# A hybrid decoder block: the products that spread the shares of the attention's groups, as pairs on half the array rows, two chunks at once

## Chip, cores and metric

The kernel runs on one core of one Trainium2 chip. The metric is the device time of one execution in microseconds, the median of three runs. The core has five engines, each with an instruction queue of its own that is worked in order: TensorE (PE, matrix products), VectorE (DVE), ScalarE (ACT), GpSimd (POOL) and SyncE (SP), which here only issues DMAs.

## The reference

One decoder layer in float32 over a sequence of 2048 positions and a width of 1024. The part that matters here is the combination of the attention's three groups, which differ in window and dilation:

```python
for g, (window, dilation) in enumerate(DILATION_GROUPS):        # (128,1), (512,4), (2048,16)
    o_g, lse_g = dilated_band_attention(q[:, :, g], k[:, :, g], v[:, :, g], window, dilation)
...
wts = jax.nn.softmax(jnp.stack(lses, axis=0), axis=0)           # over the groups: the shares
attn = jnp.sum(wts[..., None] * jnp.stack(outs, axis=0), axis=0)
attn = attn.reshape(B, S, ATTN_OUT_WIDTH).astype(dt) * jax.nn.silu(g_attn)
y_a = attn @ w_attn_proj[l]
```

Each of the 8 heads of a group has 64 channels. Beside it a second branch (convolution, gated recurrence) ends in `y_b = (h * silu(g_lru)) @ w_lru_proj`; both are gated, added, projected and normalised.

## The kernel before

The program has three stages: the input projection up to about 1450 us, the attention to 1775 us, and the output projections to the end. The change lies in the attention.

**Work of the attention.** Heads go in four pairs (`hp` 0 to 3), each with three units, one for each group of the reference. The 12 units have 16 blocks of 128 queries. The loop `for G in range(NG + 1)` takes four blocks a turn (`scores(2G)` and `scores(2G+1)`, two blocks each), so a unit lasts four turns. The text calls a turn of this loop a group, and "short" one where the blocks have no previous block of keys: 8 transposes in a turn of p instead of 16, and scores 128 wide instead of 192.

In a group, in this order: `turn_p(2G-2)` transposes the p of the group before on PE and `copy_p` brings the result from PSUM to SBUF (half e=0 by ACT, half e=1 by DVE); `scores(2G)` multiplies q and k on PE; `weigh` masks and takes the minimum on DVE, then the exponential on ACT; `scores(2G+1)`; `turn_p(2G-1)` with its copies; two more `weigh`; `values` (PE, into o) with a copy by DVE; then prefetches (`todo`). The rest of the group is filled with a product of the other branch: `yb_part(n, hf, 0..3)`, 3 products each, half an output tile yb a group. When the second half ends, `yb_done` multiplies it into gB on DVE. Groups 20 and 37 have no yb (`rests`). In every fourth group `turn_ml` transposes the minima and sums (tile mlt, PSUM buffer o).

**Shares.** When a head pair's three units are done, `weights(hp)` works out the shares from the tiles mt, on DVE, ACT and POOL, in steps set for the groups e+1 to e+4 (e is 12, 24, 36 for hp 0, 1, 2), and stores 12 rows of 2048 in DRAM (`w_scr`). In group e+6 `load_wh` fetches them, one chunk of 512 positions a DMA, into `WH[c % 2]`, which holds two chunks each.

**Spreading.** The share of a head has to stand on that head's 64 partitions. `spread(hp, c, g, tag)` does it by a product with a 0/1 matrix `sel`, 128 x 128 on 512 columns, float32r, into a PSUM tile w; DVE multiplies o by it, and one group later POOL adds (`join`), and for the last of the three g multiplies by the gate ga and stores to `at_scr`. Each head pair has 4 chunks and 3 groups g, 12 products. For hp 0 to 2 the table `spreads` sets them into the groups from e+7 on, two a group, between parts of yb, with the PSUM tags s0 and s1 that the scores have too (two buffers each). hp 3 follows in the last stage, with tag z.

**Buffers and queues.** The order on each engine is the order of the calls. The tile pool makes whoever takes a buffer wait for the last reader of what was in it. ga tiles and the raw weights wlr share six buffers (tag rc), loaded through SP's queue.

Of the kernel before, what the change touches and what calls it, by code (L numbers as in the profile page):

```python
# [8 lines left out]
F32 = mybir.dt.float32  # L9
# [6 lines left out]
P = 128  # L16
# [4 lines left out]
CH = 512  # L21
# [10 lines left out]
def hybrid_block_kernel(ctx: ExitStack, tc: tile.TileContext, a: dict, out: bass.AP):  # L32
    nc = tc.nc
    sp, act, dve, pool, pe = nc.sync, nc.scalar, nc.vector, nc.gpsimd, nc.tensor

    def flat(t):
        return t.bitcast(F32)
# [6 lines left out]
    w_scr = [dram.tile([12, S], F32, name=f"w_scr{hp}") for hp in range(HP)]  # L44
# [59 lines left out]
    cur = {}  # L104
# [8 lines left out]
    def later(lag, fn):  # L113
        late.append((now["n"] + lag, fn))
# [4 lines left out]
    def run(queue):  # L119
        due = [x for x in queue if x[0] <= now["n"]]  # L120
        queue[:] = [x for x in queue if x[0] > now["n"]]
        for _, fn in due:
            fn()
# [21 lines left out]
    ps = stA.enter_context(tc.tile_pool(name="ps", bufs=2, space=PSUM))  # L145
# [93 lines left out]
    def tt(eng, out, in0, in1, op):  # L239
        eng.tensor_tensor(out=out, in0=in0, in1=in1, op=op)  # L240
# [70 lines left out]
    lo_, up_ = slice(0, 64), slice(64, P)  # L311
# [263 lines left out]
    base = [sum(ticks[:s]) for s in range(NQ + 1)]  # L575
# [137 lines left out]
    for s, pl in enumerate(plan):  # L713
        if pl[0] and pl[4] == "ug":
            i = pl[1][1][0] - FT_U
# [210 lines left out]
    sel = w_p.tile([P, 2, 3, P], F32R, name="sel")  # L926
    WH = [w_p.tile([P, CH], F32R, name=f"wh{i}") for i in range(2)]
# [3 lines left out]
    aps = stB.enter_context(tc.tile_pool(name="aps", bufs=2, space=PSUM, reuse_waits="tile"))  # L931
# [3 lines left out]
    def rc(name):  # L935
        return rc_p.tile([P, CH], F32, tag="rc", name=name, bufs=6)
# [17 lines left out]
    def selectors():  # L954
        for r in range(2):
            t = rc(f"self{r}")[:, 0:3 * P].rearrange("p (g f) -> p g f", g=3)
            pool.memset(t, 0.0)
            for g in range(3):
                for x in range(2):
                    v = t[:, g].rearrange("p (h f) -> p h f", h=2)  # L960
                    pool.affine_select(out=v, in_=v, pattern=[[-1, 2], [0, 64]], compare_op=ALU.not_equal, fill=1.0,
                                       base=-(32 * r + 6 * x + 2 * g), channel_multiplier=1)
            pool.tensor_copy(sel[:, r], t)
        for w in WH:
            pool.memset(flat(w), 0.0)
# [65 lines left out]

    def copy_p(j, e):
        ptb, pt, los = st["t", j]
        on_act = e == 0 or (j % 2 and (j + 1) // 2 in spreads)
        whole = los[0] == los[1]
        for b in (slice(0, 2),) if whole else (slice(0, 1), slice(1, 2)):
            lo = los[b.start]
            dst, src = ptb[:, b, :, 64 * e:64 * e + 64], pt[e][:, b]
            if lo:
                dst, src = (t.rearrange("p b (h x) f -> p b h x f", x=2)[:, :, :, 1, :] for t in (dst, src))  # L1040
            if on_act:
                act.activation(dst, src, AF.Copy)
            else:
                dve.tensor_copy(dst, src)
# [100 lines left out]
        return top, sums, lambda: (shares(), store())  # L1145

    def load_wh(hp, c):
        sp.dma_start(flat(WH[c % 2][32 * (c // 2):32 * (c // 2) + 12]), w_scr[hp][:, c * CH:(c + 1) * CH])

    def spread(hp, c, g, tag):  # L1150

        cs = slice(c * CH, (c + 1) * CH)
        os = [o_tile(3 * hp + UG[x])[:, cs] for x in range(3)]
        w = cur["ps"].tile([P, CH], F32, tag=tag, name=f"w{hp}{c}{g}", bufs=cur["wb"])
        pe.matmul(w, sel[:, c // 2, g], WH[c % 2], start=True, stop=True)
        tt(dve, os[g], os[g], w, ALU.mult)
        if g == 0:
            st["ga", hp, c] = rc(f"ga{hp}{c}")
            sp.dma_start(st["ga", hp, c], ga_scr[hp * P:(hp + 1) * P, cs])
            return  # L1160

        def join():
            tt(pool, os[0], os[0], os[g], ALU.add)
            if g == 1:
                tt(pool, os[0], os[0], st.pop(("ga", hp, c)), ALU.mult)
                if hp == 3 and c == CO[0]:
                    later(1, lambda: split(AT[c][:, 3, 0], AT[c][:, 3, 1], os[0]))
                else:
                    pool.dma_start(at_scr[hp * P:(hp + 1) * P, cs], os[0])

        later(1, join)
# [146 lines left out]
    for hp in range(3):  # L1318
        e = 4 * (3 * hp + 2) + 4
# [8 lines left out]
    spreads = {}  # L1328
    for hp in range(3):
        e = 4 * (3 * hp + 2) + 4  # L1330
        for i in range(12):
            c, g = i // 3, (0, 2, 1)[i % 3]
            spreads.setdefault(e + 7 + (i + (hp < 2)) // 2, []).append((hp, c, g))

    rests = set()
    for G in range(NG + 1):
        run(late)
        if G < NG:
            if G:
                turn_p(2 * G - 2)  # L1340
                copy_p(2 * G - 2, 0)
                copy_p(2 * G - 2, 1)
            scores(2 * G)
            weigh(4 * G)
            weigh(4 * G + 1)
            scores(2 * G + 1)
            if G:
                turn_p(2 * G - 1)
                copy_p(2 * G - 1, 0)
                copy_p(2 * G - 1, 1)  # L1350
            weigh(4 * G + 2)
# [12 lines left out]
        for fn in todo.pop(G, ()):  # L1364
            fn()
        y = G >= GY and G not in rests and (G < NG or len(halves) % 2)
        if y:
            n, hf = divmod(halves[0], 2)
            yb_part(n, hf, 0)
            yb_part(n, hf, 1)  # L1370
        two = spreads.pop(G, [])
        if len(two) == 2:
            spread(*two[0], "s0")
        if y:
            yb_part(n, hf, 2)
        if two:
            spread(*two[-1], "s1")
        if y:
            yb_part(n, hf, 3)
            if hf:  # L1380
                yb_done(n)
        if G % 4 == 0 and G:
            turn_ml(G // 4 - 1)
        if y:
            yb_care(halves.pop(0))
            if hf and n in (7, 15):
                rests.add(G + 1)
        now["n"] += 1
# [203 lines left out]
    for t, tt in enumerate(TT):  # L1592
        c, b = divmod(t, 4)
# [67 lines left out]
```

## Time and profile before

| | |
|---|---|
| median of 3 runs | 2114.13 us (2111.71 to 2115.91) |
| profiled execution, first to last instruction (the only time listed for it) | 2110.6 us |
| PE busy | 2092.4 us, 99% |
| DVE busy | 1645.0 us, 78% |
| ACT busy | 1212.7 us, 57% |
| POOL busy | 764.2 us, 36% |
| granted TensorE clock, mean | 0.998 |
| chain that ended last | PE 95%, DMA 2%, DVE 1%, POOL 1%, ACT 1% |
| spreading products in the attention, L1155 | 36, mean 401 ns, busy 14.1 us |
| multiplications by them on DVE | 36, median 687 ns |

A row of the order in time is: start in us, duration in us, engine, line, operation, output <- inputs, the operand's rows and columns, shape, count. Consecutive instructions of one kind are merged into one row, whose duration reaches from the first start to the last end. Matmuls overlap, so what one costs is the step from start to start. In brackets stands the idle time of the engine just before, and what ended it.

### The profile page before, as it was taken

To read this page: it belongs to the slowest core of one execution; us is meant where nothing else is said; L and a number is where in the kernel's file an instruction comes from. 1 tells how busy PE (TensorE), PEld (TensorE's weight loads), DVE (VectorE), ACT (ScalarE), POOL (GpSimd) and SP (SyncE) were. 2 spreads that over 40 slices of the span, in tenths; PEclk is the share of its full clock that TensorE was granted. 3 is DMA by queue.
4 is the path that set the end of the run, shared out by engine and by line. 5 is a ranking of instruction groups with operands and counts; after the bars stand their busy time and mean duration, and the time that the engine had idled before them with its cause. 6 is when DMAs were issued, how large, how long until landed. Compare 5 with 4: busy or idle time off the path is not lost.

```text
span 2110.6 us, 35731 instructions
## 1 busy us (share of the span) xinstructions
PE 2092.4 (99%) x12069; PEld 1713.1 (81%) x12069; DVE 1645.0 (78%) x2937; ACT 1212.7 (57%) x2510; POOL 764.2 (36%) x685
## 2 busy tenths in 40 slices
PE   9999999999999999999999999999999999999998
PEld 7888888888888888888888888887888878788886
DVE  8878988989988868677777878875667776877667
ACT  6456556567567556677677787775666664321100
POOL 1544653653653301111111111112547678521120
PEclk9999999999999999999999999999999999999999
DMA  7876976886886866566665666669879886774431
GB/s 222 245 230 196 266 227 203 255 239 208 248 256 210 301 192 181 191 205 174 206 190 175 207 205 204 188 205 275 209 208 260 233 234 184 243 243 154 152 100 70
DMA packets 259205, 443.10 MB, mean 210 GB/s; under 512 B 65504, under 2 KB 92160, under 8 KB 255952
## 3 DMA queue, kind: packets, MB, share of 16 engines
q1 hardware_dynamic: 242384, 408.38, 62.0%
q0 software_dynamic: 11744, 23.54, 6.0%
q10 hardware_dynamic: 4896, 8.92, 1.1%
q8 instruction: 96, 1.57, 0.3%
q14 instruction: 85, 0.70, 0.1%
HBM read 289.74 MB, written 150.99 MB: 209 GB/s over the span
## 4 chain that ended last, share of the span: by engine, by line
PE 95%; DMA 2%; DVE 1%; POOL 1%; ACT 1%; issue 1%; SPq 0%; ACTq 0%; POOLq 0%; DVEq 0%
PE q L639 65%; PE yb L1231 6%; PE o L1061 3%; PE z L1536 3%; PE z L1537 3%; PE z L1538 3%; PE pt L1029 2%; PE s L998 2%; PE ya L1504 1%; PE ya L1503 1%; PE ya L1505 1%; PE g L500 1%; PE vtp L370 1%; PE s L992 1%; DMA war<-in_w_f_dram 1%
## 5 line engine op out<-in xcount | busy, mean ns | idle before, releaser
L639 PE MATMUL q<-xT,hS 128*128 128x512 f32 x1632 | 505.0, 391 | 0.1
L639 PE MATMUL q<-xT,l 128*128 128x512 f32 x1088 | 423.5, 389 | 0.0
L639 PE MATMUL q<-xB,hA 128*128 128x512 f32 x1344 | 418.0, 392 | 0.0
L639 PE MATMUL q<-xB,l 128*128 128x512 f32 x944 | 367.9, 390 | 0.0
L639 PEld LDWEIGHTS q<-xT,hS 128*128 128x128 f32 x1632 | 304.6, 188 | 65.0 <-issue 2.7
L639 PEld LDWEIGHTS q<-xB,hA 128*128 128x128 f32 x1344 | 250.7, 188 | 57.0 <-issue 5.8
L639 PEld LDWEIGHTS q<-xT,l 128*128 128x128 f32 x1088 | 204.3, 188 | 42.6
L240 POOL TENSOR_TENSOR sw<-sw,sin 128x512 f32<-128x512 f32 x96 | 156.8, 1639 | 166.2 <-ACT sw L329 94.7
L639 PEld LDWEIGHTS q<-xB,l 128*128 128x128 f32 x944 | 177.5, 188 | 37.2
L240 POOL TENSOR_TENSOR y<-y,h 128x512 f32<-128x512 f32 x28 | 38.8, 1386 | 384.1 <-DVE h L541 352.1
L1014 ACT ACTIVATE pb<-pb 128x192 f32<-128x192 f32 (+1 forms) x384 | 160.7, 422 | 26.5 <-DVE pb L1012 26.4
L639 PE MATMUL q<-xB,hS 128*128 128x512 f32 x544 | 169.0, 392 | 0.0
L639 PE MATMUL q<-xT,hA 128*128 128x512 f32 x544 | 167.8, 390 | 0.0
L284 ACT ACTIVATE hA<-wA 128x512 fp32r<-128x512 f32 x220 | 138.6, 636 | 28.5 <-DVE l L240 9.1
L1231 PE MATMUL yb<-hx,wl 128*128 128x512 f32 x576 | 148.9, 400 | 0.1
L284 ACT ACTIVATE hS<-S 128x512 fp32r<-128x512 f32 x170 | 108.6, 639 | 60.7 <-DVE S L240 47.3
L240 POOL TENSOR_TENSOR l<-wA,hA 128x512 fp32r<-128x512 f32 x68 | 107.8, 1585 | 91.4 <-ACT hA L284 60.9
L1231 PEld LDWEIGHTS yb<-hx,wl 128*128 128x128 f32 x576 | 104.8, 188 | 28.4 <-issue 5.6
L639 PEld LDWEIGHTS q<-xT,hA 128*128 128x128 f32 x544 | 101.9, 188 | 21.4 <-issue 0.4
L639 PEld LDWEIGHTS q<-xB,hS 128*128 128x128 f32 x544 | 101.2, 188 | 21.5 <-issue 1.1
L240 DVE TENSOR_TENSOR S<-S,wA 128x512 f32<-128x512 f32 x102 | 96.8, 949 | 11.5 <-DMA wA<-in_w_in_dram 7.9
L1507 POOL TENSOR_TENSOR me<-gA,me 128x512 f32<-128x512 f32 x30 | 47.7, 1607 | 157.6 <-DVE gA L1506 135.3
(213 smaller groups left out, 4325.4 us busy)
## 6 DMA issues: line engine op xcount, KB each, us to landing
wA<-in_w_in_dram SPq DMA_DIRECT2D x220, 256.0 KB
wl_scr<-l SPq DMA_DIRECT2D x102, 512.0 KB
l<-wl_scr SPq DMA_DIRECT2D x102, 512.0 KB
wS<-in_w_in_dram SPq DMA_DIRECT2D x102, 256.0 KB
wS<-in_w_in_dram POOLq DMA_DIRECT2D x68, 256.0 KB, 7.0
wlr<-in_w_f_dram SPq DMA_DIRECT2D x64, 256.0 KB
mg_scr<-y SPq DMA_DIRECT2D x59, 256.0 KB
v_scr<-vs SPq DMA_DIRECT2D x48, 256.0 KB
```

The source lines that it names most:

```text
L240: eng.tensor_tensor(out=out, in0=in0, in1=in1, op=op)
L284: act.activation(heads(h), heads(r, False), AF.Copy)
L639: pe.matmul(bank, w[:, ks], x[:, kk, xx], start=(first and i == 0), stop=(last and i == 11))
L998: pe.matmul(bank[h][es, b, 0:BW], q[hs, n * P + 64 * e:n * P + 64 * e + 64], k_[hs, at + 64 * e:at + 64 * e + BW], start=True, stop=True)
L1014: act.activation(pp, pp, AF.Exp, scale=-1.0, bias=mm, accum_out=ll)
L1029: pe.transpose(pt[e][:, b, 2 * h + x, :], pdata(p, h, c, c + P)[hs], ident[hs, hs])
L1061: pe.matmul(o[hs, 2 * i + b, :], V[:, kb, 64 * h:64 * h + 64], ptb[:, b, 2 * h + x, :], start=(x == lo // P), stop=(x == 1))
L1231: pe.matmul(YB["t"], w[:, a, k], hx(8 * c + k)[:, b], start=(hf == 0 and m == 0), stop=(hf == 1 and m == 11))
L1507: (dve if i in (6, 7) else pool).tensor_tensor(out=ME[c][:, f], in0=ga, in1=ME[c][:, f], op=ALU.add)
L1536: pe.matmul(z, mh[:, k], w[:, 0, hs], start=(k == 0), stop=False)
L1537: pe.matmul(z, mh[:, k], w[:, 1, hs], start=False, stop=False)
L1538: pe.matmul(z, ml[:, k], w[:, 0, hs], start=False, stop=(k == 7))
```

## The change

```diff
             pool.affine_select(out=v, in_=v, pattern=[[-1, 2], [0, 64]], compare_op=ALU.not_equal, fill=1.0,
-                               base=-(32 * r + 6 * x + 2 * g), channel_multiplier=1)
+                               base=-(64 * r + 6 * x + 2 * g), channel_multiplier=1)
...
-        on_act = e == 0 or (j % 2 and (j + 1) // 2 in spreads)
+        on_act = e == 0 or (j % 2 and (j + 1) // 2 in shared)
...
     def load_wh(hp, c):
-        sp.dma_start(flat(WH[c % 2][32 * (c // 2):32 * (c // 2) + 12]), w_scr[hp][:, c * CH:(c + 1) * CH])
+        sp.dma_start(flat(WH[c % 2][64 * (c // 2):64 * (c // 2) + 12]), w_scr[hp][:, c * CH:(c + 1) * CH])
...
+    def spread_pair(hp, c, g):
+
+        ws = [aps.tile([P, CH], F32, tag=f"s{r}", name=f"w{hp}{c + 2 * r}{g}", bufs=2) for r in range(2)]
+        for r, hs in enumerate((lo_, up_)):
+            pe.matmul(ws[r], sel[hs, r, g], WH[c][hs], start=True, stop=True)
+        for r in range(2):
+            share(hp, c + 2 * r, g, ws[r])
...
-        for i in range(12):
-            c, g = i // 3, (0, 2, 1)[i % 3]
-            spreads.setdefault(e + 7 + (i + (hp < 2)) // 2, []).append((hp, c, g))
+        for i in range(6):
+            spreads[e + 7 + i + (hp < 2)] = (hp, i // 3, (0, 2, 1)[i % 3])
+    shared = set(spreads)
...
     for G in range(NG + 1):
         run(late)
+        if G in spreads:
+            spread_pair(*spreads.pop(G))
...
-        two = spreads.pop(G, [])
-        if len(two) == 2:
-            spread(*two[0], "s0")
-        if y:
             yb_part(n, hf, 2)
-        if two:
-            spread(*two[-1], "s1")
-        if y:
             yb_part(n, hf, 3)
```

`share` is what `spread` did after its product: the multiplication, the load of ga for g = 0, and the join. The rows of the second chunk in a WH tile move from partition 32 to partition 64, and with them the ones in `sel`. So chunks c and c+2 lie on the two halves of the array rows, and one pair of products, 64 rows each, spreads both. There are 6 pairs for each of hp 0 to 2. They stand in the groups 20 to 25, 32 to 37 and 43 to 48, each ahead of the first turn of p; the products stood in the groups 19 to 25, 31 to 37 and 43 to 48.

PE around the end of group 22 and the start of group 23. In a name like w011 the digits are hp, chunk and g; pt044 is half 0 of the turn of scores 44. Before:

```order
L1231 MATMUL yb10_16245<-hx1_13981,wl_13979 128x512 x6
L1155 MATMUL w011_16380<-wh1_13984,sel_13982 128x512
L1231 MATMUL yb10_16245<-hx1_13981,wl_13979 128x512 x3
L1155 MATMUL w020_16386<-wh0_13983,sel_13982 128x512
L1231 MATMUL yb10_16245<-hx1_13981,wl_13979 128x512 x3
L1029 MATMUL pt044_16401<-ident_161,pb_13978 128x64
```

After:

```order
L1061 MATMUL o41_16353<-ptb42_16277,V_13900 64x128 x8
L1243 MATMUL yb10_16246<-hx1_13981,wl_13979 128x512 x12
L1160 MATMUL w010_16396<-wh1_13984,sel_13982 128x512
L1160 MATMUL w030_16397<-wh1_13984,sel_13982 128x512
L1029 MATMUL pt044_16406<-ident_161,pb_13978 128x64
```

The two products left the middle of yb and stand as a pair of chunks 1 and 3 behind it, directly ahead of the turn, and so ahead of the scores of group 23.

DVE at the same place, from the copy of o in group 22 to the first weigh of group 23 (s046). Before:

```order
L1077 COPY o1_13976<-o41_16353 128x2x128 x2
L240 TENSOR_TENSOR o1_13976<-o1_13976,w011_16380 128x512
L240 TENSOR_TENSOR o2_13977<-o2_13977,w020_16386 128x512
L1241 SCALAR_TENSOR_TENSOR gB8_16072<-gB8_16072,yb10_16245 128x512
L1044 COPY ptb44_16403<-pt144_16402 128x8x64
L1012 ISA pb_13978<-s046_16422,band_171 128x192
```

After:

```order
L1077 COPY o1_13976<-o41_16353 128x2x128 x2
L1253 SCALAR_TENSOR_TENSOR gB8_16067<-gB8_16067,yb10_16246 128x512
L240 TENSOR_TENSOR o2_13977<-o2_13977,w010_16396 128x512
L240 TENSOR_TENSOR o2_13977<-o2_13977,w030_16397 128x512
L1044 COPY ptb44_16408<-pt144_16407 128x8x64
L1012 ISA pb_13978<-s046_16427,band_171 128x192
```

The two multiplications moved behind the one into gB, between it and the copy of the turn.

POOL from the last join of hp 1 to the weights of hp 2 (mt2), groups 38 and 39; ga13 is the gate of hp 1, chunk 3. Before:

```order
L240 TENSOR_TENSOR o0_13975<-o0_13975,o1_13976 128x512
L240 TENSOR_TENSOR o0_13975<-o0_13975,ga13_18000 128x512
L1169 DMA at_scr_74<-o0_13975 128x512
L1190 CAST wl_13979<-wlr170_17874 128x512
L240 TENSOR_TENSOR wl_13979<-wlr170_17874,wl_13979 128x512
L1190 CAST wl_13979<-wlr171_17875 128x512
L240 TENSOR_TENSOR wl_13979<-wlr171_17875,wl_13979 128x512
L240 TENSOR_TENSOR mt2_17316<-whl2_18138,mt2_17316 32x128
```

After:

```order
L240 TENSOR_TENSOR o0_13975<-o0_13975,o1_13976 128x512
L240 TENSOR_TENSOR o0_13975<-o0_13975,ga11_17754 128x512
L1181 DMA at_scr_74<-o0_13975 128x512
L240 TENSOR_TENSOR o0_13975<-o0_13975,o1_13976 128x512
L240 TENSOR_TENSOR o0_13975<-o0_13975,ga13_17757 128x512
L1181 DMA at_scr_74<-o0_13975 128x512
L1202 CAST wl_13979<-wlr170_17873 128x512
L240 TENSOR_TENSOR wl_13979<-wlr170_17873,wl_13979 128x512
L1202 CAST wl_13979<-wlr171_17874 128x512
L240 TENSOR_TENSOR wl_13979<-wlr171_17874,wl_13979 128x512
L240 TENSOR_TENSOR mt2_17316<-whl2_18138,mt2_17316 32x128
```

The joins of chunks 1 and 3 now follow each other here; chunk 1's stood three groups earlier.

More of the change, by code (lines that the diff above doesn't have):

```diff
@@ L1147, in load_wh, with share @@
     def load_wh(hp, c):
-        sp.dma_start(flat(WH[c % 2][32 * (c // 2):32 * (c // 2) + 12]), w_scr[hp][:, c * CH:(c + 1) * CH])
+        sp.dma_start(flat(WH[c % 2][64 * (c // 2):64 * (c // 2) + 12]), w_scr[hp][:, c * CH:(c + 1) * CH])
     def spread(hp, c, g, tag):
+        w = cur["ps"].tile([P, CH], F32, tag=tag, name=f"w{hp}{c}{g}", bufs=cur["wb"])
+        pe.matmul(w, sel[:, c // 2, g], WH[c % 2], start=True, stop=True)
+        share(hp, c, g, w)
+    def spread_pair(hp, c, g):
[4 more added lines that the diff above has]
+            share(hp, c + 2 * r, g, ws[r])
+    def share(hp, c, g, w):
         cs = slice(c * CH, (c + 1) * CH)
         os = [o_tile(3 * hp + UG[x])[:, cs] for x in range(3)]
-        w = cur["ps"].tile([P, CH], F32, tag=tag, name=f"w{hp}{c}{g}", bufs=cur["wb"])
-        pe.matmul(w, sel[:, c // 2, g], WH[c % 2], start=True, stop=True)
         tt(dve, os[g], os[g], w, ALU.mult)
```

## The prediction

> **What bounds the kernel now.** First the page's head, then the busy time by stretch, then the waits of TensorE, and only then the order of time inside the attention, where the change acts.
>
> ```profile
> span 2110.6 us, 35731 instructions
> PE 2092.4 (99%) x12069; PEld 1713.1 (81%) x12069; DVE 1645.0 (78%) x2937; ACT 1212.7 (57%) x2510; POOL 764.2 (36%) x685
> 1655.00:1705.00 50.00, 49.95 (x673) 40.35 (x668) 38.32 (x157) 35.97 (x145) 35.12 (x37) 1.00 0.95 257
> PE mlt L1082 <- DVE o L1077: 0.6, 1, 0.6
> PE pt L1029 <- ACT ptb L1042: 2.3, 3, 1.5
> ```
>
> TensorE (PE) is the bound. The third line is a stretch in the middle of the changed groups (its columns: window, length, then busy time and count of PE, weight loads, VectorE, ScalarE, GpSimd, then PE's granted clock, the DMA share, GB/s): PE is busy 49.95 of 50 us while VectorE (DVE) is busy 38.3. The last two lines are all that PE waited for DVE's and ACT's copies in the whole attention. So a product taken from PE is worth its slot, and every new wait of PE costs its full length. The sum stands against the span of 2110.6 us; the median of the runs is 2114.13, so 3.5 us lie around the span, and I add the difference to the median.
>
> Two whole groups as PE runs them, one with two spreading products, one with none, then the starts of a short group and of the group that lacks yb:
>
> ```profile
> 1592.01 1.67 PE L1231 MATMUL yb<-hx,wl 128*128 128x512 f32 x6
> 1593.52 0.39 PE L1155 MATMUL w<-wh,sel 128*128 128x512 f32 x1
> 1593.75 0.86 PE L1231 MATMUL yb<-hx,wl 128*128 128x512 f32 x3
> 1594.45 0.39 PE L1155 MATMUL w<-wh,sel 128*128 128x512 f32 x1
> 1594.68 0.84 PE L1231 MATMUL yb<-hx,wl 128*128 128x512 f32 x3
> 1595.45 0.71 PE L1029 MATMUL pt<-ident,pb 64*128 64x64 f32 x16
> 1596.09 1.53 PE L998 MATMUL s<-qk 64*64 64x192 f32 x32
> 1597.55 0.71 PE L1029 MATMUL pt<-ident,pb 64*128 64x64 f32 x16
> ...
> 1623.74 3.04 PE L1231 MATMUL yb<-hx,wl 128*128 128x512 f32 x12
> 1626.71 0.72 PE L1029 MATMUL pt<-ident,pb 64*128 64x64 f32 x16
> ...
> 1736.05 0.46 PE L1029 MATMUL pt<-ident,pb 64*128 64x64 f32 x8
> 1736.35 1.11 PE L992 MATMUL s<-qk 64*128 64x128 f32 x16
> 1737.30 0.41 PE L1029 MATMUL pt<-ident,pb 64*128 64x64 f32 x8
> ```
>
> The third column of such a row is how long the merged piece lasted; what an operation costs PE is the step between starts. From yb to the next turn is 1595.45 - 1592.01 = 3.44 us with two products and 1626.71 - 1623.74 = 2.97 us without: 0.235 us each, not the 0.39 us of the row.
>
> **Term 1, taken away.** 36 products in the attention at 0.235 us: -8.5 us, all on the path. The 12 of the last head pair stay as they are.
>
> **Term 2, added.** 18 pairs. A pair of 64-row products on 512 columns exists already, in the gates:
>
> ```profile
> 108.06 0.50 PE L500 MATMUL g<-vh,gw 64*128 64x512 f32 x2
> 108.40 0.39 PE L500 MATMUL g<-vl,gw 64*128 64x512 f32 x2
> 108.63 0.40 PE L500 MATMUL g<-vh,gw 64*128 64x512 f32 x2
> 108.95 0.74 PE L639 MATMUL q<-xB,hS 128*128 128x512 f32 x2
> ```
>
> A middle pair takes 108.63 - 108.40 = 0.23 us: its halves run side by side. The pairs next to a change of the array's layout take 0.34 and 0.32. The new pair follows yb, where the layout changes in any case, and precedes turns of the same 64*128 form, so I take 0.25 (ends 0.23 and 0.34): +4.5 us. PE alone would gain 4.0.
>
> **Term 3, the wait put in their place.** The pair takes one buffer each of s0 and s1. Each tag has two, so the order is pair, scores(2G), scores(2G+1), and scores(2G+1) gets the pair's buffers back only when DVE has multiplied both halves into o. Before, the products came after both scores, and the next use of those buffers was a whole group away. DVE's rows at such a place:
>
> ```profile
> 1593.95 0.69 DVE L240 TENSOR_TENSOR o<-o,w 128x512 f32<-128x512 f32 x1 [0.71 <-PE w L1155]
> 1775.15 1.27 DVE L240 TENSOR_TENSOR o<-o,w 128x512 f32<-128x512 f32 x2
> 1770.69 0.69 DVE L1241 SCALAR_TENSOR_TENSOR gB<-gB,yb 128x512 f32<-128x512 f32 x1
> 1771.42 0.69 DVE L1044 COPY ptb<-pt 128x512 f32<-128x512 f32 x1
> ```
>
> A multiplication starts 1593.95 - 1593.52 = 0.43 us after its product, two in a row take 1.27, and PE resumes about 0.05 later (1580.86 below, after a copy that ends at 1580.80). So the buffers are free 1.75 us after the pair starts. Where the group before ended an output of yb, the multiplication into gB goes ahead on DVE (0.43 after the last product of yb, which starts some 0.31 before the group ends, so at 0.12, then 0.73 to the next operation): 0.12 + 0.73 + 1.27 + 0.05 = 2.17 us. PE arrives there after the pair, one turn and half the scores. In a whole group that is 0.25 + 0.64 + 0.73 = 1.62 us (1595.45, 1596.09, 1597.55); in a short one 0.25 + 0.30 + 0.48 = 1.03 (1736.05, 1736.35, 1737.30); with a short turn and 192-wide scores about 1.4. The waits, without and with gB ahead: whole 0.13 and 0.55, mixed 0.35 and 0.77, short 0.72 and 1.14. By groups: G 20 short with gB, 21 mixed, 22 whole, 23 whole with gB, 24 about 0.2, 25 about 0.6: 3.0 us. G 32 short, 33 mixed with gB, then as 22 to 25: 3.0. G 43 short, 44 short with gB, 45 mixed, 46 whole with gB, 47 whole, 48 about 0.5, where the copy of the turn and the copy of o stand behind the multiplications and no yb covers them: 3.4. Sum, unrounded, +9.3 us; between 0 (DVE's answer covered) and 15 (the two multiplications not overlapped, 1.60 for 1.27 in 18 places, and the joins slowing DVE).
>
> [...]
>
> **Term 4, the two groups without yb.** In G=20 the turn of ML (mlt) waits for the copy of o, with both products as cover:
>
> ```profile
> 1579.58 0.73 PE L1155 MATMUL w<-wh,sel 128*128 128x512 f32 x2
> 1580.86 0.33 PE L1082 MATMUL mlt<-ident,pb 128*128 128x128 f32 x1 [0.55 <-DVE o L1077]
> 1579.77 1.03 DVE L1077 COPY o<-o 128x512 f32<-128x512 f32 x1
> 1578.08 0.29 DVE L1012 CUSTOM_DVE_ANT_0 pb<-s,mask 128x128 f32<-128x128 f32 x1
> ```
>
> Now DVE begins the group with gB and two multiplications (to 2.1 us), then a copy (0.5), eight pieces of weigh (1579.77 - 1578.08 = 1.7) and the copy of o (1.03): 5.3 us, while PE stands at mlt after about 4.0. A wait of 1.4 for 0.55: +0.9. In G=38, behind G=37, the second turn needs a copy that is now behind one multiplication more, 0.69, and the wait for it is not covered by yb: +0.8. Together +1.7 (ends 0.5 and 3).
>
> **Term 5, GpSimd's queue ahead of the shares of the third head pair.** Two chunks end at once, so their joins come at once and later:
>
> ```profile
> 1708.76 1.28 POOL L240 TENSOR_TENSOR o<-o,o 128x512 f32<-128x512 f32 x1
> 1710.11 1.28 POOL L240 TENSOR_TENSOR o<-o,ga 128x512 f32<-128x512 f32 x1
> 1711.69 0.57 POOL L1169 DMA_DIRECT2D at_scr<-o  x1 [0.30 <-POOL o L240]
> 1716.36 1.41 POOL L240 TENSOR_TENSOR mt<-whl,mt 32x128 f32<-32x128 f32 x3
> 1717.80 0.52 ACT L1128 ACTIVATE mt<-mt 32x384 f32<-32x384 f32 x1 [3.54 <-POOL mt L240]
> 1718.85 0.72 PE L1029 MATMUL pt<-ident,pb 64*128 64x64 f32 x16 [1.48 <-ACT ptb L1042]
> ```
>
> Here PE waits 1.48 us for a copy that ACT cannot start before its exponential of mt, which waits for GpSimd. After, a second join of 1712.26 - 1708.76 = 3.5 us stands ahead of mt. PE itself comes to G=39 about 1.4 us later, counted from G=36 (by terms 1 to 4 nothing in G=36, 0.6 in G=37, 0.8 in G=38), so +2.1 us (ends 0, if GpSimd's splits of hx ahead of them, 8 of 1.9 us, start sooner and absorb it, and 4.2, if the added add of the second chunk, 1.28, counts too and PE is later by 0.6 only).
>
> **Term 6, the shares of the third head pair are fetched too late.** For hp=2 the first product stood at the end of G=43; the pair now stands at its front and needs chunks 0 and 2.
>
> ```profile
> 1734.91 2.18 SPq L1148 DMA_DIRECT2D wh<-w_scr  x4
> 1740.17 0.39 PE L1155 MATMUL w<-wh,sel 128*128 128x512 f32 x1
> 1573.72 2.44 SPq L1202 DMA_DIRECT2D hx<-hb_scr  x4
> 1577.77 0.61 POOL L1206 CAST hx<-hx 128x512 fp32r<-128x512 f32 x1 [6.10 <-DMA hx<-hb_scr]
> ```
>
> The third of four issues leaves near 1736.0, just as G=43 begins (1736.05). No landing time of wh is shown. Below, it cannot be before its issue has ended, about 0.5 us of waiting; above, chunk 0 was there 1740.17 - 1734.91 = 5.3 us after its issue, which gives 5.2. The nearest load that somebody waited for took 1577.77 - 1573.72 = 4.05 us but is larger (128 rows of 512 against 12), so I take 3: +3.0 us. The other two head pairs have a whole group more and wait for nothing. The fetch follows GpSimd's store and that follows DVE's reciprocal of G=40, so a late PE does not hide it.
>
> **What costs nothing.** The ga loads come as pairs and take two of the six rc buffers for a group longer; SyncE then waits for joins before the next wlr, which is loaded two groups ahead of its use. If that cover goes, a wl split is late by up to 2 us. The affine_select base and the address in WH change no duration.
>
> **Sum.** -8.5 + 4.5 + 9.3 + 1.7 + 2.1 + 3.0 = +12.1 us, and 2114.1 + 12.1 = 2126.2 us. After the attention PE runs without a gap but one of half a microsecond, so nothing gives it back.
>
> **Rivals.** *The buffers are free in time, and the pairs pay.* If scores(2G+1) finds them (the point is 1.75 us after the pair's start, against PE's 1.03 to 1.62), and the shares land in time, terms 1 and 2 are left: -4.0 us, 2110.1. For it: whole groups without gB miss by only 0.13. Against: short groups and those with gB miss by 0.5 to 1.1 even with every latency rounded down. *Only the groups' own waits.* POOL's earlier splits of hx absorb the joins and wh lands within a microsecond: terms 1 to 4 and 0.5, +7.5, 2121.6. For it: nobody measured wh. *The halves do not overlap*, so a pair costs 0.47: 18 x 0.22 = 4 us more, of which the waits of 0.3 and more swallow about half: 2128. Against: the gates' 0.23. *Waits that only partly arise*: half of term 3 and no more than 1 us of terms 5 and 6, -8.5 + 4.5 + 4.65 + 1.7 + 1.0 = +3.4, 2117.5, which nobody could tell from no change.
>
> **How the numbers follow.** 0.2% of 2114 is 4.2 us, about the least that a measurement tells from none. The forecast (9 to 16 us slower) gets 0.47, the groups' own waits alone (4.3 to 9) 0.23, halves that do not overlap or waits beyond my upper ends 0.10, a gain under 4.2 either way 0.12, a gain above it 0.08. Slower 0.80, same 0.12, faster 0.08. The range leaves out about 0.1 on each side: 2117 (the partial waits) to 2132 (every unknown near its upper end, +18).
>
> **What would show it.** In the profile after: pairs that step 0.23 to 0.34 us to the turn behind them (term 2); idle time of PE before scores or weight loads of scores, released by DVE's o<-o,w, some 9 us in up to 18 places, longest in G=20 and 44 (term 3); mlt's wait of over 1 us in G=20; a wait on ACT of 3 to 4 us in G=39; one wait of PE on the load of wh before the first pair of hp=2. Scores that start right behind the turn with no wait would prove term 3 wrong, and with it the sign.

## The result, and the profile after

The changed kernel takes 2131.28 us (2130.59 to 2132.37), the kernel before, measured beside it, 2112.92: a ratio of 1.0086 [1.0073, 1.0099], so 18.4 us slower. The forecast was 12.1 us slower. The direction and most of the reasons held; 6 of the 18 us were not foreseen, and they lie in one place that was read wrongly and in a granted clock of 0.66 and 0.83 behind the two long waits, which the forecast did not have.

The page's head of the changed kernel, its busy time by stretch (the columns as before; the tenth entry, 0.66 and 0.83, is PE's granted clock), and its waits of PE in the attention (waiting instruction <- releaser: total us, times, longest):

```profile
span 2129.3 us, 35713 instructions
1655.00:1705.00 50.00, 49.80 (x605) 38.70 (x605) 34.58 (x145) 31.69 (x132) 30.32 (x31) 1.00 0.90 257
1720.00:1730.00 10.00, 7.31 (x57) 6.38 (x58) 5.59 (x22) 4.10 (x17) 4.11 (x6) 0.66 0.23 83
1750.00:1760.00 10.00, 7.81 (x64) 6.54 (x64) 4.64 (x21) 4.11 (x19) 2.15 (x4) 0.83 0.46 152
PE pt L1029 <- DVE ptb L1044: 6.1, 1, 6.1
PE w L1160 <- DMA wh<-w_scr: 2.6, 1, 2.6
PE mlt L1082 <- DVE o L1077: 1.5, 2, 1.1
PE pt L1029 <- ACT ptb L1042: 1.0, 3, 0.4
PE s L992 <- DVE o L240: 0.4, 2, 0.2
```

Three things to see. Between 1655 and 1705 us PE counts as busy for 49.80 of 50 us, almost as before (49.95), though the groups in it have become longer (below): a busy share does not show this loss. Two long waits are new, 6.1 us for a copy of DVE and 2.6 us for the shares. And in the two windows that hold them the granted clock is 0.66 and 0.83.

The same middle group in both kernels. First its start in the kernel before (the next group starts at 1595.45, shown above), then the whole group in the changed kernel:

```profile
1587.81 0.71 PE L1029 MATMUL pt<-ident,pb 64*128 64x64 f32 x16
```

```profile
1590.59 0.50 PE L1160 MATMUL w<-wh,sel 64*128 64x512 f32 x2
1590.93 0.66 PE L1029 MATMUL pt<-ident,pb 64*128 64x64 f32 x16
1591.52 1.82 PE L998 MATMUL s<-qk 64*64 64x192 f32 x32
1593.26 0.71 PE L1029 MATMUL pt<-ident,pb 64*128 64x64 f32 x16
...
1595.37 3.06 PE L1243 MATMUL yb<-hx,wl 128*128 128x512 f32 x12
1598.35 0.50 PE L1160 MATMUL w<-wh,sel 64*128 64x512 f32 x2
```

Before, 1595.45 - 1587.81 = 7.64 us; after, 1598.35 - 1590.59 = 7.76. The pair steps 0.34 us to the turn. The scores last 1.82 where 1.53 was usual: 0.29 us of waiting stands inside the merged row and is named by no view of waits.

The waits of G=20 and G=21, as PE shows them in the changed kernel:

```profile
1579.58 1.20 PE L992 MATMUL s<-qk 64*128 64x128 f32 x7 [0.20 <-DVE o L240]
1583.29 0.33 PE L1082 MATMUL mlt<-ident,pb 128*128 128x128 f32 x1 [1.13 <-DVE o L1077]
1584.22 2.07 PE L998 MATMUL s<-qk 64*64 64x192 f32 x32
```

In G=20 the second scores stop for the buffer that DVE's `o<-o,w` still reads, and mlt waits 1.13 us (0.55 before). In G=21 the scores row is 0.54 us longer than 1.53.

The long wait, in G=39: rows of PE, then of DVE, then of GpSimd in the changed kernel:

```profile
1716.37 0.27 PE L1029 MATMUL pt<-ident,pb 64*128 64x64 f32 x1
1722.69 1.11 PE L1029 MATMUL pt<-ident,pb 64*128 64x64 f32 x15 [6.05 <-DVE ptb L1044]
1723.74 3.68 PE L1061 MATMUL o<-ptb,V 128*64 128x128 f32 x32
1727.35 3.48 PE L1243 MATMUL yb<-hx,wl 128*128 128x512 f32 x12
...
1721.35 0.69 DVE L1077 COPY o<-o 128x512 f32<-128x512 f32 x1 [9.97 <-POOL wl L240]
...
1715.25 0.58 POOL L1181 DMA_DIRECT2D at_scr<-o  x1 [0.30 <-POOL o L240]
1718.76 0.56 POOL L1181 DMA_DIRECT2D at_scr<-o  x1 [0.30 <-POOL o L240]
```

PE waits for DVE's copy of ptb, and that stands in DVE's queue behind the copy of `values` into o at 1721.35, before which DVE idles 9.97 us. That copy writes the first blocks of the fourth head pair into the o tile that the second head pair used. The first of the two stores reads chunk 1 of that tile; it lands 6.0 us after its issue, at 1721.23, and the copy starts 0.12 us later. The bracket of the copy names an operation of GpSimd on wl that ended in between; in e5 below the bracket of this copy names the store (11.79 us). The joins themselves start only at 1712.29, behind GpSimd's last split of hx. Behind the wait, `values` of 32 products takes 3.68 us and yb 3.48.

The same two operations in the kernel before:

```profile
1719.50 1.97 PE L1061 MATMUL o<-ptb,V 128*64 128x128 f32 x32
1721.40 3.04 PE L1231 MATMUL yb<-hx,wl 128*128 128x512 f32 x12
```

Last, the first pair of the third head pair in the changed kernel, and SyncE's loads of the shares ahead of it:

```profile
1748.98 1.54 SPq L1148 DMA_DIRECT2D wh<-w_scr  x4
1752.19 1.17 PE L1160 MATMUL w<-wh,sel 64*128 64x512 f32 x2 [2.58 <-DMA wh<-w_scr]
```

PE waits 2.58 us, and the pair then takes 1.17 us where others take 0.50.

### The profile page after: what moved, and what is told of

It reads as the page before. It is cut to its first block, busy times and chain, and to the rows that moved or that the text cites. A ratio compares the mean times of both kernels' runs of the same rounds, so it can differ in the third digit from the quotient of the medians.

```text
span 2129.3 us, 35713 instructions
## 1 busy us (share of the span) xinstructions
PE 2101.1 (99%) x12069; PEld 1716.4 (81%) x12069; DVE 1636.9 (77%) x2939; ACT 1212.0 (57%) x2508; POOL 763.7 (36%) x685
## 4 chain that ended last, share of the span: by engine, by line
PE 92%; DMA 3%; POOL 2%; issue 1%; DVE 1%; ACT 0%; SPq 0%; ACTq 0%; POOLq 0%; DVEq 0%
PE q L639 65%; PE yb L1243 6%; PE z L1544 3%; PE z L1543 3%; PE z L1545 3%; PE o L1061 3%; PE pt L1029 2%; PE s L998 2%; PE ya L1511 1%; PE ya L1510 1%; PE ya L1512 1%; PE g L500 1%; PE vtp L370 1%; DMA hx<-hb_scr 1%; POOL hx L1219 1%
## 5 line engine op out<-in xcount | busy, mean ns | idle before, releaser
L240 POOL TENSOR_TENSOR sw<-sw,sin 128x512 f32<-128x512 f32 x96 | 156.9, 1640 | 166.2 <-ACT sw L329 94.7
```

## The experiments

All are made from the changed kernel unless the text says otherwise, and each is compared with the kernel before on its own chip (medians there 2114.27, 2114.32 and 2114.01 us). The table shows, beside time and ratio, the time of PE from one turn of ML (mlt) to a later one in each profiled run: G=20 to 36 holds 10 of the 18 pairs, 36 to 40 the long wait, 40 to 44 the first pair of hp=2. From chip to chip it is the loss against the kernel before that compares: 18.4 us for the changed kernel. The last column is one middle group, the one shown above.

| kernel | us | ratio to before | 20 to 36 | 36 to 40 | 40 to 44 | 44 to 48 | group |
|---|---|---|---|---|---|---|---|
| before | 2112.92 | | 114.47 | 28.94 | 23.75 | 27.05 | 7.64 |
| changed | 2131.28 | 1.0086 [1.0073, 1.0099] | 117.42 | 37.05 | 28.94 | 28.44 | 7.76 |
| e1_chunks | 2130.26 | 1.0069 [1.0056, 1.0082] | 117.37 | 32.27 | 26.83 | 28.42 | |
| e2_behind | 2125.47 | 1.0053 [1.0040, 1.0065] | 116.54 | 35.36 | 24.59 | 26.85 | 7.66 |
| e3_thin | 2124.28 | 1.0045 [1.0031, 1.0059] | 112.70 | 35.81 | 27.88 | 26.73 | 7.44 |
| e4_first | 2129.55 | 1.0068 [1.0056, 1.0081] | 117.36 | 37.57 | 24.60 | 28.40 | |
| e5_order | 2127.94 | 1.0061 [1.0046, 1.0075] | 120.21 | 37.20 | 23.72 | 27.06 | |
| e6_both | 2119.70 | 1.0024 [1.0015, 1.0034] | 114.25 | 33.85 | 23.71 | 26.95 | |
| e7_whole | 2132.28 | 1.0080 [1.0068, 1.0092] | 116.41 | 36.92 | 30.82 | 28.14 | 7.62 |
| e8_turn | 2125.85 | 1.0054 [1.0043, 1.0066] | 118.14 | 34.31 | 25.55 | 27.75 | |
| e9_early | 2114.93 | 1.0005 [0.9996, 1.0014] | 115.16 | 27.85 | 24.19 | 26.95 | 7.58 |
| e10_wholeb | 2116.08 | 1.0009 [1.0000, 1.0017] | 116.08 | 32.28 | 23.71 | 27.09 | 7.64 |

**e1_chunks: pair other chunks.**

```diff
-        sp.dma_start(flat(WH[c % 2][64 * (c // 2):64 * (c // 2) + 12]), w_scr[hp][:, c * CH:(c + 1) * CH])
+        sp.dma_start(flat(WH[c // 2][64 * (c % 2):64 * (c % 2) + 12]), w_scr[hp][:, c * CH:(c + 1) * CH])
...
-            share(hp, c + 2 * r, g, ws[r])
+            share(hp, 2 * c + r, g, ws[r])
```

> The changed kernel with the chunks paired as 0 with 1 and 2 with 3 in place of 0 with 2 and 1 with 3; position, pairs and multiplications stay. Theory: the 6.05 us wait of PE in G=39 (8.9 us with what follows it) is DVE's copy of the fourth head pair's first blocks into the o tile that the second head pair had, which has to wait until chunk 1 there is joined and stored; chunk 1 came last with chunk 3. Then this wait goes, and what is left is GpSimd's later mt (2 to 4 us in G=40): about -5 us against the changed kernel, 2126. The prediction's theory (the two joins in a row hold up mt, and mt holds up ACT): the joins stand as before, so the wait stays and the time is 2131.

With 0+1 and 2+3 paired, chunk 1 of the second head pair is joined and stored in G=35 and not in G=38. In its profile the wait for DVE's copy in G=39 is gone, and 36 to 40 falls from 37.05 to 32.27 us; what stands there now is a wait for ACT (the row's bracket):

```profile
1725.26 1.03 PE L1029 MATMUL pt<-ident,pb 64*128 64x64 f32 x16 [2.49 <-ACT ptb L1042]
```

In this run the wait for the shares in G=43 is 1.46 us, with a granted clock of 1.00 in 1740 to 1750 us behind it, and 40 to 44 is 2.1 us shorter too. The median fell by far less than the profiled run: the loss is 16.0 us, nearer to the rival's time than to the theory's. The profiled run was the fastest of the five, 2125.29 us, the others took 2129.11 to 2130.90 with a mean granted clock lower by 0.001 to 0.002. Which waits those had, their times alone do not show; for the o tile this profile and e5 decide, not the median.

**e2_behind: the pair behind `values`, ahead of yb.**

```diff
         run(late)
-        if G in spreads:
-            spread_pair(*spreads.pop(G))
...
         for fn in todo.pop(G, ()):
             fn()
+        if G in spreads:
+            spread_pair(*spreads.pop(G))
```

> The changed kernel with the pair moved behind the values, in front of yb; pairing and chunks stay. Theory of the buffers: scores no longer wait for the multiplications (-9 us by the prediction's term), but the array changes its layout once more for each pair (0.1 to 0.2 us, +2 to +4), and the shares of the third head pair are there in time (-3.5); the wait in G=39 stays. About -9 us: 2122. Rival: the waits come from DVE's load as a whole and not from the place; then only the -3.5 of the shares, 2128.

The waits on the pair's buffers and all but 0.43 us of that on wh go (44 to 48: 26.85 us), the long wait in G=39 stays with 6.04 us. The middle group is 7.66 us, as before the change: behind `values` a pair gains nothing. G=20 to 36 is still 2.1 us longer than before; most of it is one wait of 1.51 us for a copy of DVE in G=26, the place of the wait of G=39 one head pair earlier. The loss is 11.2 us, 7.2 less than the changed kernel's, between the theory's 9 and the rival's 3.5.

**e3_thin: DVE multiplies 16 columns of 512** for the first three head pairs, so that the buffers come free early; the shares are left out of the other columns.

```diff
-        tt(dve, os[g], os[g], w, ALU.mult)
+        n = CH if hp == 3 else 16
+        tt(dve, os[g][:, 0:n], os[g][:, 0:n], w[:, 0:n], ALU.mult)
```

> The changed kernel with the multiplications of the first three head pairs cut to 16 of 512 columns, so most of the shares are not applied; products, buffers and waits stay in place. Theory of the buffers: two multiplications take about 0.3 in place of 1.27 us, so scores(2G+1) finds its buffers in all groups but the short ones with gB ahead; the waits shrink from about 9 to 1 us, -8 us: 2123. Rival (the wait is the array's change of layout or the pair itself): no change, 2131.

The same middle group:

```profile
1587.52 0.50 PE L1160 MATMUL w<-wh,sel 64*128 64x512 f32 x2
1587.86 0.66 PE L1029 MATMUL pt<-ident,pb 64*128 64x64 f32 x16
1588.44 1.53 PE L998 MATMUL s<-qk 64*64 64x192 f32 x32
...
1594.96 0.50 PE L1160 MATMUL w<-wh,sel 64*128 64x512 f32 x2
```

The scores are back at 1.53 us and the group takes 7.44 us. So here the pair's own gain shows: 7.64 - 7.44 = 0.20 us, and over G=20 to 36 (114.47 - 112.70) / 10 = 0.18 a pair. The difference to the changed kernel, 117.42 - 112.70 = 4.7 us, is what DVE's multiplications cost PE in these ten places. The loss falls from 18.4 to 10.0 us, as the theory said (8).

**e4_first: only the pair of G=43 behind its `values`.**

```diff
-        if G in spreads:
+        if G in spreads and G != 43:
             spread_pair(*spreads.pop(G))
...
+        if G == 43:
+            spread_pair(*spreads.pop(G))
```

> The changed kernel with only the first pair of the third head pair (G=43) moved behind the values of its group, 3.3 us later. Theory: PE waits for the load of wh there, 2.6 us in the profile and some 3.5 with what follows; the load is there 3.3 us later, and the scores of this short group no longer wait either: -4 us, 2127. Rival: the wait only moves, because the store of the shares is late by more: -1 us or less, 2130.5.

```profile
1750.79 1.09 PE L1061 MATMUL o<-ptb,V 128*64 128x128 f32 x16
1751.81 0.50 PE L1160 MATMUL w<-wh,sel 64*128 64x512 f32 x2
```

No wait, and 40 to 44 falls by 4.3 us (28.94 to 24.60) for a wait of 2.58: half of the 3.4 us at half clock behind it (the 0.83 in 1750 to 1760 us of the changed kernel) gives the rest. The loss fell by 3.1 us, to 15.3, nearer to the theory than to the rival, and in the profiled run the wait of G=39 was 6.92 us, longer than in the changed kernel.

**e5_order: the kernel before, only its chunks in another order**, to see whether the long wait needs pairs at all.

```diff
-            c, g = i // 3, (0, 2, 1)[i % 3]
+            c, g = (2, 3, 0, 1)[i // 3], (0, 2, 1)[i % 3]
```

> The kernel before with one change: the chunks of the first three head pairs are spread in the order 2, 3, 0, 1 instead of 0, 1, 2, 3; no pairs, every product in its old place. Theory (the long wait in G=39 is the fourth head pair's first blocks, which are copied into the o tile of the second head pair and wait until chunk 1 there is joined and stored): chunk 1 now ends in G=37 and is joined in G=38, as in the changed kernel, so the wait of 4 to 6 us of TensorE behind VectorE's copy of ptb comes back in G=39, with a half-clock window behind it: 6 to 9 us slower than the kernel before. Rival (the wait needs the pairs, whose two joins in a row hold GpSimd's queue): one join at a time, no wait above 1.5 us, within 2 us of the kernel before.

PE, DVE and GpSimd in G=39 of this kernel, then one more wait of PE that it has in G=26:

```profile
1723.38 1.11 PE L1029 MATMUL pt<-ident,pb 64*128 64x64 f32 x15 [7.88 <-DVE ptb L1044]
...
1722.04 0.69 DVE L1077 COPY o<-o 128x512 f32<-128x512 f32 x1 [11.79 <-DMA at_scr<-o]
...
1716.67 0.57 POOL L1169 DMA_DIRECT2D at_scr<-o  x1 [0.30 <-POOL o L240]
...
1623.95 0.87 PE L998 MATMUL s<-qk 64*64 64x192 f32 x12 [3.75 <-DVE o L240]
```

The wait is there without any pair, and here the bracket of DVE's copy names the store: it was issued at 1716.67, and the copy starts 5.4 us later. 36 to 40 takes 37.20 us, like the changed kernel. The rival falls. One head pair earlier, where the third takes over the tile of the first, DVE's copy into o waits for such a store too, 6.95 us, the multiplication behind it comes late, and PE's scores wait 3.75 us for their buffer: G=20 to 36 takes 5.7 us more than before. So the loss, 13.6 us, is more than the 6 to 9 that were expected of G=39 alone.

**e6_both: e1's pairing and e2's place.**

> Chunks paired as 0 with 1 and 2 with 3, and the pair behind the values instead of in front of the turns. Theory (the three losses are separate: scores waiting for the pair's buffers, the load of wh, the o tile's chunk 1): all three are gone, a pair costs 0.34 to 0.47 us for the 0.47 of its two products, so from 2 us faster to 2 us slower than the kernel before: 2112 to 2117, and TensorE has no wait above 1.6 us in the attention. Rival (the pairs have a cost that these places do not show, clock or queue): the kernel stays at 2121 or more.

1.0024, near the middle of the two theories: the three known losses are gone, but one wait of 4.56 us is new. Rows of GpSimd, ACT and PE:

```profile
1719.84 1.40 POOL L240 TENSOR_TENSOR mt<-whl,mt 32x128 f32<-32x128 f32 x3
...
1721.27 0.52 ACT L1128 ACTIVATE mt<-mt 32x384 f32<-32x384 f32 x1 [6.59 <-POOL mt L240]
...
1722.32 1.09 PE L1029 MATMUL pt<-ident,pb 64*128 64x64 f32 x16 [4.56 <-ACT ptb L1042]
```

This is the mechanism of term 5. Beside the rows of before (1716.36, 1717.80, 1.48), mt comes 3.48 us later, ACT's exponential 3.47, and PE waits 3.08 us more. Everywhere else the kernel runs as before: 36 to 40 is 4.91 us longer, all the other columns together 0.36 shorter.

**e7_whole: at the pair's place, whole products of 128 rows.**

```diff
-        for r, hs in enumerate((lo_, up_)):
-            pe.matmul(ws[r], sel[hs, r, g], WH[c][hs], start=True, stop=True)
+        for r in range(2):
+            pe.matmul(ws[r], sel[:, r, g], WH[c], start=True, stop=True)
```

> The changed kernel with whole products of 128 rows (the other rows meet zeros of sel) at the pair's place: position and buffers are as in the changed kernel, the pairing alone is taken away. Theory (the place makes the loss, the pairing saves about 0.13 us a pair, 0.47 against 0.34): 0 to 2.5 us slower than the changed kernel, with the same waits on the buffers, wh and the o tile; from the turn of ML in G=20 to that in G=24 31.4 to 32.2 us against 31.48. Rival (the halves side by side take the two buffers at once, and that makes the waits): whole products give less wait, 3 us or more faster than the changed kernel.

```profile
1588.63 0.61 PE L1160 MATMUL w<-wh,sel 128*128 128x512 f32 x2
1589.18 0.71 PE L1029 MATMUL pt<-ident,pb 64*128 64x64 f32 x16
1589.82 1.53 PE L998 MATMUL s<-qk 64*64 64x192 f32 x32
...
1596.25 0.61 PE L1160 MATMUL w<-wh,sel 128*128 128x512 f32 x2
```

The two products take 0.55 us to the turn, the scores find their buffers, and the group takes 7.62 us against 7.76 with pairs. At this place the pairing saves nothing: what PE gains it stands waiting for DVE two rows later. The place makes the loss, as the theory said; it expected whole products to be no better group by group, and they are, by 1.0 us over G=20 to 36 (30.95 from G=20 to 24, expected 31.4 to 32.2). In 40 to 44 they lose more, since the wait for wh was 3.40 us in that run. The time is that of the changed kernel within the intervals.

**e8_turn: e1's pairing, the pair behind the second turn, ahead of `values`** (in G=48, the last, behind them).

```diff
             weigh(4 * G + 3)
+            if G in spreads:
+                spread_pair(*spreads.pop(G))
             if G:
                 values([j for j in (2 * G - 3, 2 * G - 2) if j >= 0])
```

> Chunks paired as 0 with 1 and 2 with 3, and the pair behind the group's second turn, in front of the values: the array is in the pair's layout there already, and scores have more than a group's half before they need its buffers. Theory: no wait on the pair's buffers, wh or the o tile, and a pair costs 0.23 to 0.34 us, so 2 to 4 us faster than the kernel before, 2109 to 2113, unless the pair itself waits for the weighing of the first scores (then up to 0.5 us in each short group, 3 in all). Rival (any place costs as much as two whole products, since the waits only move): within 1.5 us of the kernel with the pair behind the values, or slower.

The theory fell: 1.0054, a loss of 11.5 us and not a gain. Two of its waits of PE in the attention:

```profile
PE pt L1029 <- ACT ptb L1042: 5.3, 3, 4.4
PE w L1160 <- DVE pb L1012: 1.8, 4, 1.2
```

The pair now waits for DVE's weighing of the first scores, 1.8 us in four places, and G=20 to 36 takes 3.7 us more than before, in which some 3.4 us at half clock behind the turn of ML in G=20 are counted (a granted clock of 0.83 in 1580 to 1590 us). The long wait for ACT is e6's.

**e9_early: e6, with the pairs of the first two head pairs one group earlier.**

```diff
-            spreads[e + 7 + i + (hp < 2)] = (hp, i // 3, (0, 2, 1)[i % 3])
+            spreads[e + 7 + i] = (hp, i // 3, (0, 2, 1)[i % 3])
```

> The kernel with chunks 0 with 1 and 2 with 3 and the pair behind the values, with one change: the pairs of the first two head pairs stand one group earlier, as those of the third do already, so that the last two joins of the second head pair come in G=37 and not in G=38. In that kernel GpSimd's subtractions into mt start at 1719.84 (before: 1716.36), one join of 3.5 us later, ACT's exponential follows at 1721.27 (before: 1717.80), and TensorE waits 4.56 us for the copy behind it (before: 1.48). Theory (the second join ahead of mt makes that wait): it falls to 1.5 us or less, the half-clock window behind it goes too, 4 to 6 us faster than the kernel with the later pairs: 2113 to 2116, within 2 us of the kernel before. Rival (the wait is set by other work on GpSimd, such as its splits of wl): it stays at 3 us or more and the time within 1.5 us of 2119.7. A new wait for wh of 0.5 to 2 us in G=31 or G=19 would be seen as such.

GpSimd's subtraction and PE at the same place:

```profile
1716.63 1.41 POOL L240 TENSOR_TENSOR mt<-whl,mt 32x128 f32<-32x128 f32 x3
...
1719.12 0.71 PE L1029 MATMUL pt<-ident,pb 64*128 64x64 f32 x16 [0.92 <-ACT ptb L1042]
```

With the last joins in G=37, mt is back at 1716.63, the wait is 0.92 us and 36 to 40 takes 27.85 us, 1.1 less than before the change, which has one product there (e9 has none). Two waits for wh, 1.1 us together, are new. The time is that of the kernel before: 1.0005 [0.9996, 1.0014]. The joins as such have not left GpSimd's queue ahead of mt: in the trace GpSimd works from its first split of hx at 1690.12 to mt, 26.5 us, with no pause above 0.3 us, and the joins lie in between; in e6 the same stretch is 28.9 us (from 1690.93), with two more adds in it, 2.51 us, that e9 has done before. So the rival has its part: the splits of hx, and when their loads arrive, set this stretch too.

**e10_wholeb: e9 with e7's whole products.**

> The same with whole products of 128 rows for the pairs. A pair behind the values takes 0.43 us to yb in the trace, two whole products 0.47 where the layout does not change. Theory (behind the values the pairing itself saves next to nothing): within 1.5 us of the pairs' kernel. Rival (the pairing saves half of 36 products, 4 us): 3 us or more slower.

Its median is 1.15 us above e9's and the intervals overlap. In the middle group it takes 7.64 us, e9 7.58, so 18 pairs at this place are worth about 1.1 us by that group. The runs of both kernels spread over 8 to 9 us (2110.6 to 2119.3 and 2111.1 to 2119.5); the kernel before spreads over 5.0 us on that chip (2111.3 to 2116.3), but over 9.0 on the chip of e5 to e8 (2110.2 to 2119.2). The profiled run of e10 is one of its slowest and has the wait of e6 again:

```profile
1722.34 1.12 PE L1029 MATMUL pt<-ident,pb 64*128 64x64 f32 x16 [3.85 <-ACT ptb L1042]
```

In that run GpSimd idles 3.45 us for a load of hx and starts to split it at 1693.40, 3.3 us later than in e9; it then works as long as there, 26.5 us, and its mt comes 3.2 us later than in e9's (1719.85). That the spread of both is this wait, coming and going, is likely but seen in one run of each only. None of these versions is faster than the kernel before.

## Why the prediction was right or wrong

At 2131.28 us the time lies 0.7 below the upper end of the stated range, and that is luck: the kernel before, measured beside it, took 1.2 us less than the 2114.13 from which the forecast counts. The 18.4 us themselves are beyond the 9 to 16 of the main forecast. The direction and terms 1 to 3 are no luck; term 4 is in part, and the miss lies in terms 5 and 6.

By the starts of the groups in both traces, the groups of the change take 18.7 us more (18.4 in the medians): 7.3 in G=39 and 40, 4.3 at the first pair of the third head pair, and 7.1 in all the other groups.

**Terms 1 and 2: right in sign, 0.8 us too good.** The pair's step was put at 0.25; it is 0.34 (1590.93 - 1590.59), the upper end, as for the gates' pairs next to a change of the array's layout; each pair stands alone there, none in a run of pairs. The turn behind it is 0.05 us shorter (0.59 for 0.64). e3 shows the net gain that is left: 0.18 us a pair, 3.2 in all, for the 4.0 of the text.

**Term 3: right, mechanism and size.** The difference between the changed kernel and e3 is 4.7 us from G=20 to 36, 1.0 from 16 to 20, 1.1 from 40 to 44, 1.7 from 44 to 48 and 0.5 in G=37 (5.12 and 4.62): 9.0 us (from 16 to 20: 22.50 and 21.48), forecast 9.3. But the text said where to see it wrongly: the views of waits list 0.4 us of it, and the rest lies inside merged rows of scores that became longer. DVE's reading set the pace here: a middle group went from 7.64 to 7.76 us though PE's own work fell (by 0.20 us in e3's group), and to 7.44 when DVE read 16 columns (e3). But with whole products at the same place (e7) G=20 to 36 is 1.9 us longer than before the change, with pairs 2.9, so most of the loss is the place and not the packing.

**Term 4: right in sign, 0.7 us too much, and in G=38 for another reason.** mlt waits 1.13 us for 0.55 (forecast 1.4), and G=38 is 0.4 longer (0.8). The text put both down to DVE's longer queue, but with DVE's multiplications cut to 16 columns mlt still waits 1.17 us and G=38 is as long (8.23 us in e3, 8.22 in the changed kernel, 7.83 before). By the order of PE's rows the products are gone in both places that stood behind `values` and covered a copy; in G=38 PE now waits in the first turn and not the second, and by the profile for ACT (0.21 us). With the gain of 3.2 and the 9.0 above these make 6.8 of the 7.1 us of the ordinary groups; terms 1 to 4 gave 7.0.

**Term 5: the step that failed.** Forecast 2.1 us, measured 7.3. The text followed the two joins to what stands behind them in GpSimd's queue, and that was correct: e6 has the delay of mt to a fiftieth of a microsecond (3.48 for 3.5). It did not ask who waits for what the joins themselves produce. The store of chunk 1 moved from G=35 to G=38, and the o tile that it reads is written again by `values` of G=38. DVE's queue stops there, 9.97 us, ACT and PE with it, ahead of the wait that the text looked at; the two do not add up, the longer one is seen. The wait of 3 to 4 us for ACT that the text named as a sign is not there (its longest is 0.4). e1 removed the wait in its profiled run by another pairing, and e5 made it in the kernel before by an order of chunks. Nor did the text have the right group: the 1.48 us of before stand in G=40.

**Term 6: right, and the clock made it larger.** The wait is 2.58 us, forecast 3.0. Its removal was worth 4.3 (e4), since PE ran at half clock behind it (0.50 from 1752.3 to 1755.6 us, 1.00 from 1755.8 to 1760).

**Half clock behind long waits: not in the forecast.** It said that "every new wait of PE costs its full length". The two long ones cost more. In 1720 to 1730 us the clock of 0.66 is 6.8 us at half speed (0.50 from 1721.6 to 1728.3, 1.00 from 1728.5 to 1732), in 1750 to 1760 the 0.83 is 3.4. In G=39 the half-speed rows are longer than those of before by 1.71 (3.68 for 1.97) and 0.44 (3.48 for 3.04), and the rest of the turn, 15 transposes in 1.11, by about 0.4; with the wait less the old one, 6.05 - 1.48, that gives 7.1 of the 7.3 us. At G=43, 2.58 and half of 3.4 give the 4.3. This part is an addition to the sum, and the forecast put it at nothing.

**The rivals.** "The buffers are free in time" fell with the longer scores, "the halves do not overlap" with the step of 0.34. "Only the groups' own waits" is what would have come out without G=39 and 43: 7.1 us, for 7.5 in the text.

## What to carry to other kernels

When a step moves, follow its output as well as its queue: list who next writes the buffer that its last reader, here a store, still holds, and in which group. Work taken from the bound engine is worth something only if the slower engine that hands the buffers back keeps up at that very place (the middle group took 7.76 us with pairs, 7.44 once DVE read 16 columns); measure this by the time from group to group, since a wait inside merged rows shows in neither the busy share nor the list of waits. A sum of waits is a lower bound where the clock drops behind them: G=39 and 40 lost 7.3 us for 4.6 us of added wait.

## What the runs showed of the hardware

Behind the long waits of PE the granted clock was lower. In the changed kernel it is 0.50 from 1721.6 to 1728.3 us (the wait of 6.05 us ends at 1722.69) and 0.50 from 1752.3 to 1755.6 us (the one of 2.58 ends at 1752.19); from 1728.5 to 1732 and from 1755.8 to 1760 us it is 1.00. The wait of 2.58 us thus cost some 4.3, an estimate from the 0.83 in 1750 to 1760 us: 3.4 us at half clock, half of that on top. The profiled runs show, for the waits of PE of 1.4 us and more from G=20 on and for two shorter ones (a dash where the clock of that stretch was not read; `values` of 32 products takes 1.97 us in the kernel before, mlt 0.33, an undisturbed pair 0.50):

| run | wait of PE, us | granted clock, in the stretch (us) | a row behind the wait, us |
|---|---|---|---|
| before | 1.48 | 1.00 (1710 to 1730) | `values` 1.97 |
| changed | 6.05 | 0.66 (1720 to 1730) | `values` 3.68 |
| changed | 2.58 | 0.83 (1750 to 1760) | pair 1.17 |
| changed | 1.13 | 1.00 (1580 to 1590) | mlt 0.33 |
| e1_chunks | 2.49 | 0.83 (1720 to 1730) | `values` 3.22 |
| e1_chunks | 1.46 | 1.00 (1740 to 1750) | pair 0.65 |
| e2_behind | 6.04 | 0.73, 0.93 (1710 to 1720, 1720 to 1730) | `values` 2.88 |
| e2_behind | 1.51 | 1.00 (1630 to 1640) | `values` 1.97 |
| e3_thin | 5.28 | 0.66 (1710 to 1720) | `values` 3.68 |
| e3_thin | 2.56 | 0.83 (1740 to 1750) | pair 1.13 |
| e4_first | 6.92 | 0.66 (1720 to 1730) | `values` 3.68 |
| e5_order | 7.88 | - | `values` 3.26 |
| e5_order | 3.75 | - | `values` 3.08 |
| e6_both | 4.56 | 0.83 (1720 to 1730) | `values` 3.15 |
| e7_whole | 6.38 | - | `values` 3.68 |
| e7_whole | 3.40 | - | two whole products 1.19 |
| e8_turn | 4.42 | - | `values` 3.68 |
| e8_turn | 1.45 | 0.83 (1580 to 1590) | mlt 0.48 |
| e9_early | 0.92 | 1.00 (1710 to 1730) | `values` 1.97 |
| e10_wholeb | 3.85 | - | `values` 3.05 |
| e10_wholeb | 1.65 | - | yb 2.88 |

The length of the wait alone does not order these rows: 1.45 us in e8 stands beside 0.83, 1.46 in e1 and 1.51 in e2 beside 1.00. What else decides is not shown. Two rows of the stretch 1720 to 1730 us, of e6 (a wait of 4.56) and of e9 (0.92):

```profile
1720.00:1730.00 10.00, 7.68 (x73) 6.61 (x75) 3.84 (x19) 4.94 (x20) 4.82 (x10) 0.83 0.76 186
```

```profile
1720.00:1730.00 10.00, 10.00 (x111) 8.45 (x108) 6.47 (x31) 6.74 (x32) 6.34 (x15) 1.00 0.92 215
```

Also new: a pair of 64-row products on 512 columns stepped 0.34 us in front of the turns (changed kernel) and 0.43 between `values` and yb (e6; two whole products there: 0.58 in e10), against 0.23 within a run of pairs (the gates):

```profile
1592.37 0.50 PE L1160 MATMUL w<-wh,sel 64*128 64x512 f32 x2
1592.80 3.01 PE L1243 MATMUL yb<-hx,wl 128*128 128x512 f32 x12
```

```profile
1591.98 0.74 PE L1160 MATMUL w<-wh,sel 128*128 128x512 f32 x2
1592.56 2.93 PE L1243 MATMUL yb<-hx,wl 128*128 128x512 f32 x12
```

The first two rows are of e6, the last two of e10.
